# Hi and lo parts of the stationary weights interleaved, and activation blocks at a pitch of 2112 bytes

## The chip, the cores and the metric

The kernel runs on one core of one Trainium2 chip. The metric is the time of the kernel on the device in microseconds. Before the change it is 1505.89 us, the median of three runs (1504.97 to 1506.43).

## The reference

A decoder trunk of two layers over 512 positions and 1024 features, all in float32. Layer 0 mixes the tokens by dilated sliding-window attention in three groups of heads, layer 1 by a gated linear recurrence (RG-LRU). A gated ConvFFN follows each mixer, and every part stands between two RMS norms.

```python
def conv_ffn(x, w_up, conv_w, conv_b, w_down):
    u = causal_dwconv(x @ w_up, conv_w, conv_b)
    g, v = u[..., :D_FF], u[..., D_FF:]
    return (jax.nn.gelu(g, approximate=True) * v) @ w_down

for layer in range(DEPTH):
    h = rms_norm(x, norm_mix_pre[layer])
    h = attention(h) if layer % 2 == 0 else rglru_mixer(h)
    x = x + rms_norm(h, norm_mix_post[layer])
    h = conv_ffn(rms_norm(x, norm_ffn_pre[layer]), ...)
    x = x + rms_norm(h, norm_ffn_post[layer])
```

Nearly all of the arithmetic is in the products with the large weight matrices: `attn_w_qkv` (1024 x 9216), `attn_w_o`, `lru_w_in` (1024 x 2048), `lru_w_out`, and for each layer `ffn_w_up` (1024 x 6144) and `ffn_w_down` (3072 x 1024).

## The kernel before

**Split products.** To keep float32 accuracy at the pace of the type float32r, each operand is split into a part `hi`, which is the value rounded to float32r, and a part `lo`, the rest. `split` (line 145) does it for 512 columns at a time: ScalarE writes hi (line 146), and VectorE subtracts hi from the raw value and writes lo (line 147). A product is then three matmuls into the same bank of PSUM (`mm3`, line 245): hi with hi (line 246), hi with lo (line 247) and lo with hi (line 248). Each matmul loads its stationary operand, 128 x 128, anew; the profile lists these loads as LDWEIGHTS of the engine PEld. Small products, such as the scores of the attention, are plain float32 matmuls.

**Weights.** `plan` lists the chunks of the weights in the order of their use. `load` (line 187) fetches a chunk by DMA on SyncE's queue into one of three `raw` buffers, and `pump` (line 164) splits it into units of 128 x 1024, of which eight are alive at a time (`W_UNITS`). Until the change a unit is two tiles of the pool `wp`, tagged `hi` and `lo`, each of 4096 bytes in a partition. `pump` is called from `tick`, after every group of matmuls, and so the splits run ahead of the matmuls that use them. There are four kinds of unit:

- `feat`: 8 blocks of 128 input rows by 128 output columns. It is the stationary operand, and hT streams past it (`feat`, line 356): the result has features on the partitions and the 512 positions along the bank. It serves the queries and keys, `lru_w_in` and `ffn_w_up`: 80 chunks of two units, with 24 matmuls a unit (48 of 256 columns where the first tiles of a stage are done in halves).
- `gate`: the weights of the two gates of the recurrence, also stationary (`gates`, line 846); four units.
- `value`: two blocks of 512 columns. It streams, and hT is the stationary operand (`values`): the result v has positions on the partitions.
- `rows`: one block of 1024 columns. It streams, and the activation, split into `ahi` and `alo`, is stationary (`rows_run`, line 408): the result `acc` goes to the norms.

**Activations.** `new_hT` (line 277) makes the two tensors hT0 (hi) and hT1 (lo) in the pool `htp`: 8 blocks of 512 positions, 2048 bytes a block and 16384 bytes a tensor in each partition. `transposed` (line 293) fills them with the normed activation: TensorE transposes, ScalarE writes hi, VectorE writes lo.

**Other things on the path.** The attention's biases are laid out by GpSimd's queue: a row of biases goes to DRAM, is written 128 times over into `skew` there, and the `toe` tiles are read from it with a shifted pitch. In the recurrent layer `decay` is a chain of ScalarE, GpSimd and VectorE that ends in a scan; the projection that follows needs its result. The pools follow each other in the memory: `cp` (constants, the residual stream `x_sb`), then `htp`, `wp`, `gp` (28 general tiles of 2048 bytes) and `sp`.

Of the kernel before, what the change touches and what calls it, by code (L numbers as in the profile page):

```python
# [12 lines left out]
F32R = mybir.dt.float32r  # L13
# [5 lines left out]
P = 128  # L19
S = 512  # L20
D = 1024
KD = D // P
# [12 lines left out]
GEN_BUFS = 28  # L35
TOE_BUFS = 2
CP_PAD = 8

SHORT_ORDER = [
    ([0, 1], [0, 1, 2]), ([0], [3]), ([2, 3], [0]), ([1], [3]), ([2, 3], [1]), ([2], [2, 3]), ([3], [2, 3]),  # L40
# [36 lines left out]
def kernel(  # L77
# [29 lines left out]
    nc = tc.nc  # L107
    ctx.enter_context(tc.manual_schedule())
    cp = ctx.enter_context(tc.tile_pool(name="cp", bufs=1))
    cp.tile([P, CP_PAD], F32, tag="pad", name="pad")  # L110
    htp = ctx.enter_context(tc.tile_pool(name="htp", bufs=1))
    wp = ctx.enter_context(tc.tile_pool(name="wp", bufs=W_UNITS))
# [7 lines left out]
    def nm(s):  # L120
        uid[0] += 1
        return f"{s}{uid[0]}"
# [22 lines left out]
    def split(hi, lo, raw):  # L145
        nc.scalar.activation(hi, raw, AF.Copy)  # L146
        nc.vector.tensor_tensor(lo, raw, hi.bitcast(F32), op=ALU.subtract)  # L147

    plan = []
# [4 lines left out]
    def parts_of(kind, raw):  # L154

        if kind == "feat":
            return [raw[:, :, m * P : (m + 1) * P] for m in range(2)]
        if kind == "value":
            return [raw[:, 2 * i : 2 * i + 2, :] for i in range(2)]
        if kind == "rows":  # L160
            return [raw[:, i : i + 1, :] for i in range(2)]
        return [raw]

    def pump(limit=2):

        for _ in range(limit):
            i = state["cv"]
            if not pieces and i < state["dma"]:
                pieces.extend((i, j, u) for j, u in enumerate(parts_of(plan[i][0], raws.pop(i))))
                state["cv"] += 1  # L170
            if pieces and state["live"] < W_UNITS:
                i, j, raw = pieces.pop(0)
                hi, lo = (
                    wp.tile([P] + list(raw.shape[1:]), F32R, tag=t, name=nm("w" + t)) for t in ("hi", "lo")
                )
                h = raw.shape[1] // 2
                cuts = [(slice(None), slice(0, h)), (slice(None), slice(h, 2 * h))]
                if raw.shape[1] == 1:
                    cuts = [(slice(None), slice(0, 1), slice(n, n + 512)) for n in (0, 512)]
                for c in cuts:  # L180
                    split(hi[c], lo[c], raw[c])
                units[i, j] = (hi, lo)
                state["live"] += 1
            while not pieces and state["dma"] < len(plan) and state["dma"] - state["cv"] < RAW_BUFS:
                load()

    def load():
        i = state["dma"]
        kind, kd, cols, srcs = plan[i]
        raw = wp.tile([P, kd, cols], F32, tag="raw", name=nm("raw"), bufs=RAW_BUFS)  # L190
        at = 0
        for src, n in srcs:
            nc.sync.dma_start(raw[:, :, at : at + n] if kind == "value" else raw[:, at : at + n, :], src)
            at += n
        raws[i] = raw
        state["dma"] += 1
# [6 lines left out]
    def take(i, j):  # L203
        while (i, j) not in units:
            before = state["live"]
            pump(1)
            assert before != state["live"]
        return units[i, j]
# [7 lines left out]
    def tick():  # L216
        for s in list(sides):
            s[0] -= 1
            if s[0] <= 0:
                try:  # L220
                    s[0] = next(s[1])
                except StopIteration:
                    sides.remove(s)
        if not state["hold"]:
            pump(1 if state["live"] >= W_UNITS - 2 else 2)
# [49 lines left out]
        return [ap[:, 0:512], ap[:, 512:1024]]  # L275

    def new_hT():
        return tuple(htp.tile([P, KD, S], F32R, tag=f"hT{i}", name=nm(f"hT{i}")) for i in range(2))

    def prenorm(t, hT, g, wait):  # L280
        xh, gh = halves(x_sb[:, t, :]), halves(g)
# [126 lines left out]
    def rows_run(nchunks, A, prep, seq, order, post, pre):  # L408
        post_g = gain(*post)
        pre_g, hT = (gain(*pre), new_hT()) if pre is not None else (None, None)  # L410
        W, banks = {}, {}
        left = {}
# [93 lines left out]
    def ffn(layer, hT, post, pre):  # L506
        ca, cc = ffn_cols[layer]

        def conv(ps, j):
            u = gen(s="u")  # L510
            nc.scalar.activation(  # L511
                u, ps, AF.Identity, scale=cc[:, j : j + 1], bias=cc[:, 48 + j : 49 + j]
            )
            for d, wc in ((1, ca[:, 48 + j : 49 + j]), (2, ca[:, j : j + 1])):
                nc.vector.scalar_tensor_tensor(  # L515
                    u[:, d:], ps[:, : S - d], wc, u[:, d:], op0=ALU.mult, op1=ALU.add
                )
            return u

        gv = []  # L520

        def sink(b, ps, j):
            m = b % 2
            if b < 2:
                u = conv(ps, 2 * j + m)
                nc.scalar.activation(u, u, AF.Gelu_apprx_tanh)  # L526
                gv.append(u)
            else:
                u = conv(ps, 24 + 2 * j + m)
                nc.vector.tensor_tensor(gv[2 * j + m], gv[2 * j + m], u, op=ALU.mult)  # L530

        order = [([0, 1, 2, 3], range(9)), ([0], range(9, 12)), ([1], range(9, 12))]
        order += [([2, 3], [9]), ([2], [10, 11]), ([3], [10, 11])]
        prep, run = rows_proj(12, act_split(gv), order, post, pre)
        for j in range(12):
            if j == 11:
                prep(3)
            feat_tiles(2, hT, lambda b, ps: sink(b, ps, j), j == 0)
        return run()
# [286 lines left out]
    def lru(hT, post, pre):  # L826
# [40 lines left out]
        def decay(ns):  # L867

            js = [2 * n + m for n in ns for m in range(2)]
            at = {}  # L870
            for j in js:
                r = rs[j // 2][j % 2]
                a, th = gen(s="a"), gen(s="th")
                nc.scalar.activation(a, r, AF.Exp, scale=c8[:, j : j + 1])
                nc.scalar.activation(th, r, AF.Tanh, scale=c8[:, j : j + 1])
                nc.gpsimd.tensor_tensor(r, a, a, op=ALU.mult)
                at[j] = (a, th, r)
            for j in js:
                a, th, sq = at[j]
                nc.vector.scalar_tensor_tensor(th, sq, 1.0, th, op0=ALU.add, op1=ALU.mult)  # L880
                nc.vector.tensor_scalar(th, th, -1.0, 0.0, op0=ALU.mult, op1=ALU.max)
            pump(1)
            for j in js:
                nc.scalar.activation(at[j][1], at[j][1], AF.Sqrt)
            for j in js:
                a, th, _ = at[j]
                nc.vector.tensor_tensor(th, th, xb[j], op=ALU.mult)
                nc.vector.tensor_tensor_scan(th, a, th, 0.0, op0=ALU.mult, op1=ALU.add)
                hs.append(th)
                gate(j)  # L890
# [58 lines left out]

    root_table()  # L950
    hT = new_hT()
    nc.sync.dma_start(x_sb[:, 0, :], x[0, 0:P, :])
    g = gain(norm_mix_pre, 0, nc.sync)
# [27 lines left out]
    hT = attention(hT, (norm_mix_post, 0), (norm_ffn_pre, 0))  # L981
    hT = ffn(0, hT, (norm_ffn_post, 0), (norm_mix_pre, 1))
    hT = lru(hT, (norm_mix_post, 1), (norm_ffn_pre, 1))
# [30 lines left out]
```

## Time and profile before

| | |
|---|---|
| runs | 1504.97, 1506.43, 1505.89 us |
| profiled execution | 1504.94 us, of which the span of its instructions is 1503.2 us |
| granted clock of TensorE, mean | 0.995 |
| busy: TensorE, its weight loads | 1475.1 us, 1238.4 us |
| busy: VectorE, ScalarE, GpSimd | 799.3 us, 631.9 us, 53.8 us |
| moved by DMA | 157.65 MB, mean 105 GB/s |

The profile is one execution on the chip. A line of its groups gives the source line, the engine, the operation, what it writes and reads by the program's names without buffer numbers, the shape and the count; then the busy time in us and the mean of one in ns, and the idle time of the engine before them with what ended it. In the names, `ps<-hT,whi` is a matmul that writes the tile `ps` from hT and the hi part of a weight unit; `v<-whi,hT` and `acc<-whi,ahi` are the products of the `value` and `rows` kinds. Matmuls are pipelined: the duration of one reaches into the next, so the pace is read from the distance of their starts. In the timeline the first two columns are the start and the duration in us, and equal neighbours are merged with a count.

### The profile page before, as it was taken

The numbers are of one execution on the slowest core, as the hardware profiler recorded it, in microseconds if no ns is written. First come the engines' busy times: TensorE is split into PE (matmuls) and PEld (weight loads), VectorE is DVE, ScalarE is ACT, GpSimd is POOL, SyncE is SP. The second block draws the span as 40 slices with busy tenths as digits, with TensorE's granted clock in tenths as the row PEclk, the third lists the DMA queues.
The fourth block names the chain that finished last, engine by engine and source line by source line (L and its number), as shares of the span: only waits on it lengthen the run. The fifth ranks groups of instructions, "written<-read, shape, count | busy, mean of one in ns | idle before, by whom it ended". The sixth has DMA issues, their size and how long they took to land.

```text
span 1503.2 us, 18136 instructions
## 1 busy us (share of the span) xinstructions
PE 1475.1 (98%) x7083; PEld 1238.4 (82%) x7083; DVE 799.3 (53%) x1610; ACT 631.9 (42%) x1281; POOL 53.8 (4%) x81
## 2 busy tenths in 40 slices
PE   6999999999999999999999999999899999999998
PEld 4788888888888898888888888988698888888886
DVE  5434334343434686555565337868776555565333
ACT  5334333333333554344344234578554334444321
POOL 3021000000000000000000000003000000000000
PEclk9999999999999999999999999999999999999999
DMA  6543222424233324232233321252223232323301
GB/s 214 183 164 97 92 88 84 140 92 134 98 126 130 111 95 138 85 110 86 92 105 112 109 88 43 71 168 83 86 96 115 85 112 84 112 85 114 110 1 56
DMA packets 116102, 157.65 MB, mean 105 GB/s; under 512 B 5087, under 2 KB 97463, under 8 KB 116016
## 3 DMA queue, kind: packets, MB, share of 16 engines
q1 hardware_dynamic: 111120, 145.24, 29.1%
q0 software_dynamic: 4896, 11.26, 2.2%
q8 instruction: 55, 0.90, 0.3%
q14 instruction: 31, 0.25, 0.0%
HBM read 150.14 MB, written 11.05 MB: 107 GB/s over the span
## 4 chain that ended last, share of the span: by engine, by line
PE 95%; DVE 2%; issue 1%; DMA 1%; POOL 0%; ACT 0%; DVEq 0%; SPq 0%; POOLq 0%; ACTq 0%
PE ps L246 19%; PE ps L247 19%; PE ps L248 19%; PE acc L248 8%; PE acc L246 8%; PE acc L247 7%; PE v L246 3%; PE v L248 3%; PE v L247 3%; PE tr L297 1%; PE O L770 1%; PE S L712 1%; DVE wlo L147 1%; PE O L697 1%; PE S L662 1%
## 5 line engine op out<-in xcount | busy, mean ns | idle before, releaser
L246 PE MATMUL ps<-hT,whi 128*128 128x512 f32 (+1 forms) x1376 | 518.5, 377 | 0.0
L248 PE MATMUL ps<-hT,wlo 128*128 128x512 f32 (+1 forms) x1376 | 515.2, 374 | 0.0
L247 PE MATMUL ps<-hT,whi 128*128 128x512 f32 (+1 forms) x1376 | 515.1, 374 | 0.0
L147 DVE TENSOR_TENSOR wlo<-raw,whi 128x512 fp32r<-128x512 f32 x504 | 327.9, 697 | 276.5 <-ACT whi L146 276.3
L146 ACT ACTIVATE whi<-raw 128x512 fp32r<-128x512 f32 x504 | 285.0, 622 | 135.3 <-PE acc L248 120.9
L246 PEld LDWEIGHTS ps<-hT,whi 128*128 128x128 f32 x1376 | 259.1, 188 | 47.2 <-ACT qk L588 0.6
L248 PEld LDWEIGHTS ps<-hT,wlo 128*128 128x128 f32 x1376 | 259.0, 188 | 46.4
L247 PEld LDWEIGHTS ps<-hT,whi 128*128 128x128 f32 x1376 | 259.1, 188 | 45.6
L515 DVE SCALAR_TENSOR_TENSOR u<-ps,cols,u 128x511 f32<-128x511 f32 x192 | 143.8, 749 | 140.4 <-ACT u L511 137.0
L248 PE MATMUL acc<-whi,alo 128*128 128x512 f32 x512 | 200.0, 391 | 4.2 <-DVE alo L147 4.2
L246 PE MATMUL acc<-whi,ahi 128*128 128x512 f32 x512 | 200.6, 392 | 1.4 <-ACT ahi L146 1.4
L247 PE MATMUL acc<-wlo,ahi 128*128 128x512 f32 x512 | 199.7, 390 | 0.0
L511 ACT ACTIVATE u<-ps,cols 128x512 f32<-128x512 f32 x96 | 74.8, 780 | 209.8 <-PE ps L248 209.8
L248 PEld LDWEIGHTS acc<-whi,alo 128*128 128x128 f32 x512 | 96.5, 188 | 24.9 <-DVE alo L147 4.7
L246 PEld LDWEIGHTS acc<-whi,ahi 128*128 128x128 f32 x512 | 96.5, 188 | 21.5 <-ACT ahi L146 1.8
L247 PEld LDWEIGHTS acc<-wlo,ahi 128*128 128x128 f32 x512 | 96.4, 188 | 19.7
L247 PE MATMUL v<-wlo,hT 128*128 128x512 f32 x192 | 76.3, 398 | 3.3 <-DVE wlo L147 3.3
L246 PE MATMUL v<-whi,hT 128*128 128x512 f32 x192 | 78.0, 406 | 0.0
L248 PE MATMUL v<-whi,hT 128*128 128x512 f32 x192 | 75.9, 395 | 0.0
L526 ACT ACTIVATE u<-u 128x512 f32<-128x512 f32 x48 | 30.3, 632 | 80.7 <-DVE u L515 80.7
L649 DVE CUSTOM_DVE_ANT_0 L<-S,toe 128x128 f32<-128x128 f32 (+1 forms) x96 | 25.2, 321 | 52.7 <-DMA toe<-skew 21.9
L588 ACT ACTIVATE qk<-ps 128x512 f32<-128x512 f32 x24 | 14.3, 597 | 88.7 <-PE ps L248 76.9
(167 smaller groups left out, 1040.6 us busy)
## 6 DMA issues: line engine op xcount, KB each, us to landing
raw<-in_ffn_w_up_dram SPq DMA_DIRECT2D x48, 1024.0 KB, 5.2
raw<-in_attn_w_qkv_dram SPq DMA_DIRECT2D x28, 1024.0 KB, 5.0
raw<-in_ffn_w_down_dram SPq DMA_DIRECT2D x24, 1024.0 KB, 4.9
raw<-in_attn_w_qkv_dram SPq DMA_DIRECT2D x16, 512.0 KB, 4.9
raw<-in_lru_w_in_dram SPq DMA_DIRECT2D x8, 1024.0 KB, 5.5
skew<-rowv POOLq DMA_DIRECT2D x3, 1536.0 KB, 12.2
vrows<-v SPq DMA_DIRECT2D x16, 256.0 KB, 2.9
vp<-vrows SPq DMA_DIRECT2D x16, 256.0 KB, 4.2
```

The costliest lines, as they stand in the source:

```text
L146: nc.scalar.activation(hi, raw, AF.Copy)
L147: nc.vector.tensor_tensor(lo, raw, hi.bitcast(F32), op=ALU.subtract)
L246: mm(dst, l[0], r[0], start=start, stop=False)
L247: mm(dst, l[0], r[1], start=False, stop=False)
L248: mm(dst, l[1], r[0], start=False, stop=stop)
L297: nc.tensor.transpose(ps[:, k * P : (k + 1) * P], xs[i][:, k * P : (k + 1) * P], ident)
L511: nc.scalar.activation(u, ps, AF.Identity, scale=cc[:, j : j + 1], bias=cc[:, 48 + j : 49 + j])
L515: nc.vector.scalar_tensor_tensor(u[:, d:], ps[:, : S - d], wc, u[:, d:], op0=ALU.mult, op1=ALU.add)
L526: nc.scalar.activation(u, u, AF.Gelu_apprx_tanh)
L649: nc.vector.tensor_tensor_reduce(dst, ps, bias, scale=1.0, scalar=3 * NEG, op0=ALU.add, op1=ALU.max, accum_out=mx)
L662: mm(Sp[a // 2][:, o + lo : o + 256], q[hh][:, a * P : (a + 1) * P], k[hh][:, k0 : (a + 1) * P], start=True, stop=True)
L697: mm(po[:, a * P : (a + 1) * P], pts[a, j], vtile(v, a - 1 + j, h % 4), start=j == js[0], stop=j == 1)
```

## The change

Three edits. In `pump`, hi and lo of a unit become one tile of 8192 bytes. For the kinds `feat` and `gate` they alternate word by word: hi of column c lies at 8c bytes, lo at 8c + 4, and a block of 128 columns takes 1024 bytes. For `value` and `rows` hi fills the first half of the tile and lo the second, each in a row as before.

In `new_hT` the blocks of 512 positions stand 2112 bytes apart instead of 2048 (`HT_STEP`, 16 words). The second tensor gets another 1024 bytes at its end (`HT_GAP`, 256 words), so that both together take 34816 bytes, 17 times 2048, where they took 32768.

To make room, the memory that is set aside for the descriptors of GpSimd's DMAs is set to 8192 bytes.

```diff
+HT_STEP = 16
+HT_GAP = 256
...
             if pieces and state["live"] < W_UNITS:
                 i, j, raw = pieces.pop(0)
-                hi, lo = (
-                    wp.tile([P] + list(raw.shape[1:]), F32R, tag=t, name=nm("w" + t)) for t in ("hi", "lo")
-                )
+                n, m = raw.shape[1:]
+                both = wp.tile([P, 2 * n * m], F32R, tag="hl", name=nm("whl"))
+                if plan[i][0] in ("feat", "gate"):
+                    both = both.rearrange("p (k c t) -> p t k c", k=n, t=2)
+                else:
+                    both = both.rearrange("p (t k c) -> p t k c", k=n, t=2)
+                hi, lo = both[:, 0], both[:, 1]
...
     def new_hT():
-        return tuple(htp.tile([P, KD, S], F32R, tag=f"hT{i}", name=nm(f"hT{i}")) for i in range(2))
+        pitch = S + HT_STEP
+        both = []
+        for i in range(2):
+            t = htp.tile([P, KD * pitch + HT_GAP * i], F32R, tag=f"hT{i}", name=nm(f"hT{i}"))
+            both.append(t[:, : KD * pitch].rearrange("p (k s) -> p k s", k=KD)[:, :, :S])
+        return tuple(both)
...
-    nc = _bacc.Bacc("TRN2", target_bir_lowering=False, num_devices=1)
+    nc = _bacc.Bacc("TRN2", target_bir_lowering=False, num_devices=1, dynamic_dma_scratch_size=8192)
```

## The prediction, as it was put down before the result

> **What bounds the kernel now.** I read the page first: engines, chain, costliest groups. Then the groups by line with shapes kept apart, the timeline of one dense stretch, and the waits.
>
> ```profile
> span 1503.2 us, 18136 instructions
> PE 1475.1 (98%) x7083; PEld 1238.4 (82%) x7083; DVE 799.3 (53%) x1610; ACT 631.9 (42%) x1281; POOL 53.8 (4%) x81
> PE 95%; DVE 2%; issue 1%; DMA 1%; POOL 0%; ACT 0%; DVEq 0%; SPq 0%; POOLq 0%; ACTq 0%
> ...
> L147 DVE TENSOR_TENSOR wlo<-raw,whi 128x512 fp32r<-128x512 f32 x504 | 327.9, 697 | 276.5 <-ACT whi L146 276.3
> L146 ACT ACTIVATE whi<-raw 128x512 fp32r<-128x512 f32 x504 | 285.0, 622 | 135.3 <-PE acc L248 120.9
> ```
>
> TensorE carries 95% of the chain that ended last. VectorE and ScalarE have about half of the span free. So the change is worth what it does to the distance from one matmul's start to the next, and the durations don't give that, because matmuls overlap. The groups say which kinds there are, and the timeline gives the distance.
>
> ```profile
> L246 PE MATMUL ps<-hT,whi 128*128 128x512 f32 x1184 | 463.7, 392 | 0.0
> L248 PE MATMUL ps<-hT,wlo 128*128 128x512 f32 x1184 | 460.9, 389 | 0.0
> L247 PE MATMUL ps<-hT,whi 128*128 128x512 f32 x1184 | 460.8, 389 | 0.0
> ...
> L247 PE MATMUL v<-wlo,hT 128*128 128x512 f32 x192 | 76.3, 398 | 3.3 <-DVE wlo L147 3.3
> ...
> L246 PE MATMUL ps<-hT,whi 128*128 128x256 f32 x192 | 54.8, 285 | 0.0
> ...
> L246 PE MATMUL gate<-xhi,whi 128*128 128x512 f32 x32 | 12.4, 389 | 0.0
> ...
> L662 PE MATMUL S<-qk,qk 128*128 128x256 f32 x48 | 11.7, 380 | 0.0
> ```
>
> ```profile
> 203.68 1.14 ACT L146 ACTIVATE whi<-raw 128x512 fp32r<-128x512 f32 x2
> ...
> 203.96 0.39 PE L247 MATMUL ps<-hT,whi 128*128 128x512 f32 x1
> ...
> 204.19 0.39 PE L248 MATMUL ps<-hT,wlo 128*128 128x512 f32 x1
> 204.19 0.19 PEld L246 LDWEIGHTS ps<-hT,whi 128*128 128x128 f32 x1
> 204.34 1.29 DVE L147 TENSOR_TENSOR wlo<-raw,whi 128x512 fp32r<-128x512 f32 x2 [0.58 <-ACT whi L146]
> ...
> 206.23 0.39 PE L248 MATMUL ps<-hT,wlo 128*128 128x512 f32 x1
> ...
> 208.27 0.39 PE L248 MATMUL ps<-hT,wlo 128*128 128x512 f32 x1
> ...
> 208.50 1.72 PE L697 MATMUL O<-v,PT 128*128 128x128 f32 x14
> ```
>
> ```profile
> 940.02 0.28 PE L248 MATMUL ps<-hT,wlo 128*128 128x256 f32 x1
> ...
> 941.82 0.28 PE L248 MATMUL ps<-hT,wlo 128*128 128x256 f32 x1
> ```
>
> From 203.96 to 208.27 lie 19 distances: 0.2268 us each. From 940.02 to 941.82 lie 15: 0.120 us for 256 columns. The second 256 columns therefore cost 0.1068 us, 0.417 ns each, and what doesn't depend on columns is 226.8 - 213.6 = **13.2 ns in every matmul of a split pair**. The next weight load starts with the matmul (both 204.19) and lies inside it. This surplus is the only thing in the dense stretches that the change could take away.
>
> Is it fixed? Three places say no.
>
> ```profile
> 158.64 1.68 PE L662 MATMUL S<-qk,qk 128*128 128x128 f32 x8
> ```
>
> ```profile
> 27.74 0.63 PE L246 MATMUL v<-whi,hT 128*128 128x512 f32 x1
> ...
> 29.87 0.63 PE L248 MATMUL v<-whi,hT 128*128 128x512 f32 x1
> ```
>
> ```profile
> 27.10:30.50 3.40, 3.40 (x9) 2.72 (x9) 2.63 (x10) 1.29 (x3) 0.00 (x0) 0.50 0.00 0
> ```
>
> ```profile
> 281.51 0.40 PE L247 MATMUL ps<-hT,whi 128*128 128x512 f32 x1
> ...
> 283.59 0.39 PE L247 MATMUL ps<-hT,whi 128*128 128x512 f32 x1
> ```
>
> First, plain float32 matmuls. The 14 of 128 columns at 208.50 take (1.72 - 0.28) / 13 = 0.111 us each. The eight at 158.64 are two of 128 and six of 256; less the last one's 0.38 and two at 0.111, five remain: 0.216 us for 256 columns, which is 512 column times (213.6) and 2 ns. They stream at half the pace and pay 2, not 13. Second, at granted clock 0.50 (third figure from the end of the window's row) the split kind goes five distances in 2.13 us: 0.426 us, 512 columns at 0.833 ns with nothing left over; a fixed count of array cycles would have doubled instead. Third, after short matmuls the same instruction needs (283.59 - 281.51) / 9 = 0.231 us until it settles at 0.227. So the surplus appears only where 512 columns stream at full pace beside a weight load, and depends on how the two lie to each other: I read it as the load and the stream getting in each other's way. Against a general shortage of memory speaks that 203.96 to 206.23 (ACT and DVE at work) and 206.23 to 208.27 (neither) give the same distance.
>
> **The change part by part.**
>
> *Weights 8 bytes from column to column.* It touches the matmuls whose weights are whi or wlo: 3 x 1184 of 512 columns, 3 x 192 of 256, 3 x 32 gates; 3648 long and 576 short. The 128 weights now span 1024 bytes where they spanned 512, so a load walks through memory as many bytes per matmul column as the stream does, which is how the float32 matmuls lie (one weight column per moving column time). No row shows a weight load at this pitch. Upper bound of the gain: the surplus falls to the 2 ns of the float32 row, 226.8 to 215.6, so 3648 x 11.2 = 40.9 us; the short ones fall from 120 to the 111 ns at which loads follow each other in the L697 row, 576 x 9 = 5.2 us. Other end: the load now covers twice the bytes, and the surplus doubles, 4224 x 13.2 = 55.8 us lost. I take the first, being nearest to a row in which both walk at one pace; it stays the largest uncertainty.
>
> *Blocks at 2112 bytes, and a gap of 1024 behind the second tensor.* Every block of hT starts 64 bytes later against the weights than the one before. Stream and load of all kinds (ps, v, gate) now start at distances that are multiples of 512 bytes, and all settle at the same 0.227, so the trace can't tell what a shift does. The v matmuls, 576, use hT as weights at the old 4 bytes: between 0.231 (the unsettled row; +2.4 us) and 0.2156 (-6.5 us); I take nothing.
>
> *Strided writes and reads of the split.* Of the 504 weight splits 328 (80 column chunks x 4 and 4 gates x 2) now write, and on VectorE also read, every second word. The nearest rows:
>
> ```profile
> L776 ACT ACTIVATE oT<-O 128x512 f32<-128x512 f32 x8 | 8.8, 1100 | 39.7 <-PE O L770 34.0 <-issue 5.8
> ...
> L753 ACT ACTIVATE PT<-PT 128x512 f32<-128x512 f32 x16 | 8.6, 590 | 0.0
> ```
>
> Line 776 writes words 16 bytes apart and takes 1100 ns; line 753 writes them in a row, 590. So the price is between 0 and 510 ns a split, at most 328 x 0.51 = 167 us on ScalarE (then 799 of 1503) and as much on VectorE (then 966). The Trainium skill, "SBUF — State Buffer", section "Specifications (TRN2)", states 16-byte lines that need two hits each for full rate: by it the row at 16 bytes pays and a pitch of 8 does not, so 0. Either way it lies beside matmuls (columns: stretch, its length, then busy time and count of PE, PEld, DVE, ACT, POOL, then granted clock, DMA share, GB/s):
>
> ```profile
> 556.00:780.00 224.00, 224.00 (x1023) 186.94 (x1023) 131.16 (x192) 93.05 (x152) 0.00 (x0) 1.00 0.31 103
> ...
> 960.00:1070.00 110.00, 104.36 (x458) 85.83 (x457) 85.13 (x122) 76.13 (x120) 11.42 (x10) 0.98 0.35 115
> ```
>
> In the first ConvFFN (556 to 780) VectorE has 93 us free and DMA is at 0.31; matmuls faster by 5% need no more than that. In the recurrent layer (960 to 1070) TensorE idles 5.6 us because the chain of decay ends late there. Between the last gates and the projection stand three chunks, 144 matmuls: what they gain the wait takes back, 144 x 11.2 = 1.6 us. If that cover is gone, the eight to sixteen splits there cost up to 0.51 us each on VectorE, 4 to 8 us.
>
> *One tile for hi and lo.* A matmul that reads hi might now wait for lo's write too, one L147 (0.7 us) later. All of TensorE's later work would queue behind it; but units are prepared ahead, and TensorE's list of waits has none for the ps matmuls:
>
> ```profile
> PE tr L297 <- ACT xs L330: 10.3, 1, 10.3
> PE acc L248 <- DVE alo L147: 4.2, 1, 4.2
> PE v L247 <- DVE wlo L147: 3.3, 5, 0.7
> ```
>
> So 0. *The smaller scratch for DMA descriptors* touches POOL's queue. The three skew writes (1536 KB, 12.2 us to landing) are followed by the toe loads, for which VectorE waits 21.9 us and TensorE never. Queued behind them are the loads of the constants; I take 0.
>
> ```profile
> skew<-rowv POOLq DMA_DIRECT2D x3, 1536.0 KB, 12.2
> ...
> DVE L L649 <- DMA toe<-skew: 21.9, 2, 12.6
> ```
>
> **Sum**, against the profiled execution's 1504.94 (span 1503.2 and 1.7 around it): -40.9 - 5.2 + 1.6 = -44.5, so 1460.4. The median of the runs lies 0.95 above that execution: 1461.4, given as **1462**.
>
> **The rivals.**
>
> *The surplus doesn't depend on addresses.* What the load takes would be counted in columns, 128 whatever their pitch. For: it is equal in ps, v, gate. Against: all of these had like distances. Nothing moves: **1505**. The Trainium skill, "TensorE: Matmul & The Clock Gate", section "Step-by-step: what each phase is for", speaks for this and against the change: TensorE has two independent read ports, and loading the next weights takes no read bandwidth from the running matmul. The trace agrees that a load lies wholly inside a matmul, not that it is free: 13.2 ns remain at full pace.
>
> *Bytes touched are what counts* (the slower side). The surplus would be one piece per stretch of memory that the load opens; 1024 bytes instead of 512 double it from 13.2 to 26.4 in 4224 matmuls: 1504.9 + 55.8 + 1.0, **1561**. For: at clock 0.50 the surplus vanishes although load and stream slow down together, so their ratio of bytes is unchanged; a shortage of reading does that, a mismatch of paces alone does not. And strided access costs double in line 776. Against: ACT's and DVE's reading changes nothing. It decides as soon as the distance of ps matmuls lies above 0.2268.
>
> *Only the strided splits are felt*, TensorE's pace unchanged: the recurrent layer's 4 to 8 us, **1509 to 1514**.
>
> **How the numbers follow.** Surplus gone or mostly gone (half would be 1483): 0.45. No dependence: 0.27. Bytes touched: 0.16. Strided splits, or a shift that unsettles v (+2.4): 0.12. About 0.2% (3 us) can be told from no change. Faster is the first case and 0.03 of the second, 0.48; same 0.24; slower the last two, 0.28. The range takes in the first, second and fourth, 0.84, from 1457 (the upper bound with v's gain in part) to 1514. The likeliest case alone: 1457 to 1484.
>
> **What would show it.** Right: ps matmuls 0.216 apart in dense stretches, 0.111 to 0.112 for 256 columns, acc unchanged at 0.227, weight loads no longer than 0.19; L146 and L147 near 622 and 697. Wrong: 0.227 (no dependence), 0.240 (bytes touched), or L146 towards 1100 with TensorE waiting for whi. Also wrong, if v moves as much as ps: then the pitch of hT counted, not that of the weights.

## The result, and the profile after

The changed kernel takes **1525.45 us** (1524.93 to 1526.18, four runs) against 1505.83 us for the kernel before: a ratio of **1.0131**, 95% interval 1.0116 to 1.0146. It is slower by 19.6 us. The forecast was 1462 us, faster, with a range of 1457 to 1514.

The page of the changed kernel: engines, the chain that ended last, the weight splits.

```profile
span 1523.1 us, 18135 instructions
PE 1496.4 (98%) x7083; PEld 1264.5 (83%) x7083; DVE 799.4 (52%) x1610; ACT 642.1 (42%) x1281; POOL 54.0 (4%) x81
PE 95%; DVE 2%; issue 1%; DMA 1%; POOL 0%; ACT 0%; DVEq 0%; SPq 0%; POOLq 0%; ACTq 0%
...
L149 DVE TENSOR_TENSOR whl<-raw,whl 128x512 fp32r<-128x512 f32 x504 | 327.9, 697 | 281.9 <-ACT whl L148 281.5
L148 ACT ACTIVATE whl<-raw 128x512 fp32r<-128x512 f32 x504 | 296.2, 649 | 136.7 <-PE acc L254 120.9
L252 PEld LDWEIGHTS ps<-hT,whl 128*128 128x128 f32 x1376 | 267.5, 194 | 46.7 <-ACT qk L599 0.6
```

The span grew by 19.9 us and TensorE's busy time by 21.3, with the same count of matmuls, so TensorE idles no more than before. VectorE's time is the same, and ScalarE's 10 us more lie beside TensorE. So the matmuls themselves stand further apart. To see by how much, take 180 us of the first ConvFFN in which TensorE runs without a gap and only ps matmuls of 512 columns are issued. The window's row gives the stretch, its length, then busy time and count of TensorE; the first is of the kernel before, asked for TensorE alone, the second of the changed one, with PEld, DVE, ACT and POOL behind. At the end stand granted clock, DMA share and GB/s.

```profile
580.00:760.00 180.00, 180.00 (x796) 1.00 0.30 97
```

```profile
580.00:760.00 180.00, 180.00 (x777) 151.07 (x776) 101.13 (x148) 72.09 (x115) 0.00 (x0) 1.00 0.29 95
```

A matmul counts when its 0.39 us touch the window, so the distance is 180.39 / 796 = **226.6 ns** before and 180.39 / 777 = **232.2 ns** after. Over all starts of a kind in the trace, pauses (distances over 1.25 times the usual one) left out, the means are:

| distance in ns | count | before | after |
|---|---|---|---|
| ps, 512 columns | 3552 | 226.9 | 232.2 |
| ps, 256 columns | 576 | 119.8 | 119.8 |
| gate | 96 | 226.7 | 233.2 |
| v (hT is the weight) | 576 | 227.7 | 231.9 |
| acc (neither changed) | 1535 | 226.9 | 226.9 |

3552 x 5.3 + 576 x 4.2 + 96 x 6.5 = 21.9 us, close to the 21.3 us by which the busy time grew. The row of v matters: its weights are at 4 bytes as before, only the pitch of hT is new. The gates are the opposite: their stream is no part of hT, only their weights are new. Both got slower, so both halves of the change seemed to cost. How the distances follow each other inside a unit says more (medians by place in the unit, 24 places, worked out from the starts):

```
before  227 at every place
after   230 233 233 229 235 232 230 236 229 237 233 229 | 230 233 233 229 235 232 230 236 229 237 233 229
```

Before, a unit settles at one value. After, it runs through a pattern that comes back every 12 matmuls, which are four blocks; and over four blocks the stream moves by 4 x 64 = 256 bytes against the weights, if multiples of 1024 are left out.

### The profile page after: what moved, and what is told of

Its sections match the earlier page's. It is cut to its first block, busy times and chain, and to the rows that moved or that the text cites. A ratio compares the mean times of both kernels' runs of the same rounds, so it can differ in the third digit from the quotient of the medians.

```text
span 1523.1 us, 18135 instructions
## 1 busy us (share of the span) xinstructions
PE 1496.4 (98%) x7083; PEld 1264.5 (83%) x7083; DVE 799.4 (52%) x1610; ACT 642.1 (42%) x1281; POOL 54.0 (4%) x81
## 4 chain that ended last, share of the span: by engine, by line
PE 95%; DVE 2%; issue 1%; DMA 1%; POOL 0%; ACT 0%; DVEq 0%; SPq 0%; POOLq 0%; ACTq 0%
PE ps L253 19%; PE ps L252 19%; PE ps L254 19%; PE acc L254 7%; PE acc L252 7%; PE acc L253 7%; PE v L252 3%; PE v L253 3%; PE v L254 3%; PE tr L308 1%; PE S L723 1%; PE O L781 1%; DVE whl L149 1%; PE O L708 1%; PE S L673 1%
## 5 line engine op out<-in xcount | busy, mean ns | idle before, releaser
L252 PE MATMUL ps<-hT,whl 128*128 128x512 f32 (+1 forms) x1376 | 524.1, 381 | 0.0
L253 PE MATMUL ps<-hT,whl 128*128 128x512 f32 (+1 forms) x1376 | 522.1, 379 | 0.0
L254 PE MATMUL ps<-hT,whl 128*128 128x512 f32 (+1 forms) x1376 | 519.9, 378 | 0.0
L149 DVE TENSOR_TENSOR whl<-raw,whl 128x512 fp32r<-128x512 f32 x504 | 327.9, 697 | 281.9 <-ACT whl L148 281.5
L148 ACT ACTIVATE whl<-raw 128x512 fp32r<-128x512 f32 x504 | 296.2, 649 | 136.7 <-PE acc L254 120.9
L252 PEld LDWEIGHTS ps<-hT,whl 128*128 128x128 f32 x1376 | 267.5, 194 | 46.7 <-ACT qk L599 0.6
L253 PEld LDWEIGHTS ps<-hT,whl 128*128 128x128 f32 x1376 | 269.5, 196 | 43.5
L254 PEld LDWEIGHTS ps<-hT,whl 128*128 128x128 f32 x1376 | 268.8, 195 | 42.1
L254 PE MATMUL acc<-whl,alo 128*128 128x512 f32 x512 | 200.2, 391 | 4.2 <-DVE alo L149 4.2
L252 PE MATMUL acc<-whl,ahi 128*128 128x512 f32 x512 | 200.8, 392 | 0.5 <-ACT ahi L148 0.5
L253 PE MATMUL acc<-whl,ahi 128*128 128x512 f32 x512 | 199.8, 390 | 0.0
L254 PEld LDWEIGHTS acc<-whl,alo 128*128 128x128 f32 x512 | 96.6, 189 | 24.8 <-DVE alo L149 4.7
L252 PEld LDWEIGHTS acc<-whl,ahi 128*128 128x128 f32 x512 | 96.6, 189 | 20.8 <-ACT ahi L148 1.0
L253 PEld LDWEIGHTS acc<-whl,ahi 128*128 128x128 f32 x512 | 96.6, 189 | 19.8
L253 PE MATMUL v<-whl,hT 128*128 128x512 f32 x192 | 76.9, 401 | 2.8 <-DVE whl L149 2.8
L252 PE MATMUL v<-whl,hT 128*128 128x512 f32 x192 | 78.5, 409 | 0.0
L254 PE MATMUL v<-whl,hT 128*128 128x512 f32 x192 | 76.0, 396 | 0.0
```

Source lines behind the costliest of these rows:

```text
L252: mm(dst, l[0], r[0], start=start, stop=False)
L253: mm(dst, l[0], r[1], start=False, stop=False)
L254: mm(dst, l[1], r[0], start=False, stop=stop)
```

## The experiments

Two theories stood at first. **A**: weights at 8 bytes cost by themselves, because the load opens 1024 bytes instead of 512. **B**: the 64-byte steps of hT cost, because load and stream never settle.

**The halves of the change, each alone, and a control.** `interleave_only` keeps hT and the descriptor memory as before. `pitch_only` keeps hi and lo in a row, and `one_tile` does so with hT as before.

```diff
 # interleave_only
-HT_STEP = 16
-HT_GAP = 256
+HT_STEP = 0
+HT_GAP = 0
...
-... num_devices=1, dynamic_dma_scratch_size=8192)
+... num_devices=1)
 # pitch_only
-                if plan[i][0] in ("feat", "gate"):
+                if plan[i][0] in ():
 # one_tile: as pitch_only, and HT_STEP = 0, HT_GAP = 0
```

> Weights interleaved as in the changed kernel; hT at 2048 bytes and the descriptor memory as before. Theory A (the 8-byte weights themselves cost, because the load opens 1024 bytes instead of 512): ps matmuls 231 to 234 ns apart, v back at 227.7, the time 17 to 19 us above before, about 1523. Theory B (what costs is that the blocks of hT stand 64 bytes further against the weights at each step, so that load and stream never settle): ps at 227, only the 96 gate matmuls at 233, about 1506.

> hT at 2112 bytes with the gap and the smaller descriptor memory; hi and lo one after the other in one tile for all kinds of unit. Theory A: ps at 227, v at 232, so 2 to 3 us above before, about 1508. Theory B: ps and v at 231 to 233, about 1523, gates at 227.

> Control: only the one tile for hi and lo (one after the other) and the smaller descriptor memory, hT at 2048 bytes. Both theories: all split matmuls at 227, within 2 us of before, 1504 to 1508.

| kernel | us | ratio to before (95%) | ps | gate | v |
|---|---|---|---|---|---|
| interleave_only | 1533.34 | 1.0183 (1.0166 to 1.0200) | 234.9 | 235.6 | 227.9 |
| pitch_only | 1522.89 | 1.0115 (1.0100 to 1.0130) | 231.8 | 227.3 | 231.7 |
| one_tile | 1506.39 | 1.0003 (0.9994 to 1.0013) | 226.9 | 226.7 | 227.7 |

The same window, first of interleave_only, then of pitch_only:

```profile
580.00:760.00 180.00, 180.00 (x766) 150.21 (x765) 99.84 (x146) 70.34 (x112) 0.00 (x0) 1.00 0.30 96
```

```profile
580.00:760.00 180.00, 180.00 (x779) 145.93 (x778) 100.97 (x148) 69.92 (x116) 0.00 (x0) 1.00 0.29 95
```

766 and 779 matmuls where before had 796. Both theories are half right, and neither expected the whole: each half alone slows the kernel, by 27.9 and 17.5 us (A had expected 17 to 19 for the first, B 17 for the second), and both together cost 19.6, less than the interleaving alone. They don't add up. The short matmuls lose next to nothing: 120.0 ns with the interleaving alone, and 118.4 with the pitch alone. The one tile and the smaller descriptor memory cost nothing.

**A table of paces.** To see what the distance depends on, a small kernel leaves the trunk out and issues series of 24 split-type matmuls with the same two operands, from one tile.

```diff
+STEPS = (1, 2)
+OFFS = (0, 4, 8, 16, 24, 32, 48, 64, 80, 96, 112, 128, 160, 192, 224, 256, 384, 512)
...
+    def series(count, w_at, step, m_at):
...
+        for n in range(count):
+            w, m = w_at(n), m_at(n)
+            mm(ps, fill[:, w : w + 127 * step + 1 : step], fill[:, m : m + 512], start=n == 0, stop=n == count - 1)
...
+    M0 = 4096
+    same = lambda v: lambda n: v
...
+    for step in STEPS:
+        for off in OFFS:
+            series(24, same(0), step, same(M0 + off))
```

All of these count in words of 4 bytes: `w` and `m` are the starts of weights and stream, `step` the pitch of the weights.

> A kernel that leaves the whole trunk out: series of split-type matmuls of 512 columns from one tile, weights always at its start, 4 or 8 bytes from column to column, the stream at 18 starts of 16384 + 0 to 2048 bytes; then four series in the order of a ps unit (both weight pitches, blocks at 2048 and 2112). Theory A: every series at 4 bytes about 227 ns apart, every series at 8 bytes 230 to 240, whatever the start. Theory B: both pitches spread by more than 4 ns over the starts, and of the four unit series those with 2112 are slow. If neither start nor pitch matters in the table (all 227), the cost comes from changing addresses between one matmul and the next.

The timeline merges a series into one row: start, duration, count. The name of the target is the series; the granted clock is 1.00.

```profile
24.87 5.60 PE L129 MATMUL rab<-fill 128*128 128x512 f32 x24
30.31 5.72 PE L129 MATMUL rac<-fill 128*128 128x512 f32 x24
35.87 5.77 PE L129 MATMUL rad<-fill 128*128 128x512 f32 x24
...
52.58 5.76 PE L129 MATMUL rag<-fill 128*128 128x512 f32 x24
...
63.77 5.62 PE L129 MATMUL rai<-fill 128*128 128x512 f32 x24
...
85.93 5.62 PE L129 MATMUL ram<-fill 128*128 128x512 f32 x24
...
124.37 5.76 PE L129 MATMUL rat<-fill 128*128 128x512 f32 x24
...
224.79 16.49 PE L129 MATMUL rbl<-fill 128*128 128x512 f32 x72
241.11 16.86 PE L129 MATMUL rbm<-fill 128*128 128x512 f32 x72
257.81 16.95 PE L129 MATMUL rbn<-fill 128*128 128x512 f32 x72
274.60 16.89 PE L129 MATMUL rbo<-fill 128*128 128x512 f32 x72
```

A row's duration less the last matmul's 0.39, over 23 distances: with weights at 4 bytes and the stream 16384 + 0, 16, 32, 128, 256 and 512 bytes behind them (rab, rac, rad, rag, rai, ram) 226.5, 231.7, 233.9, 233.5, 227.4 and 227.4 ns. The two at 256 and 512 begin a little slower and settle at 226.7. So do those at 768, 1024, 1536 and 2048; every other start of the table, from 16 to 896 bytes, ends between 228.9 and 233.3. This is the new theory, **C: with weights at 4 bytes the pace depends on the distance of stream and weights modulo 256 bytes, and a multiple of 256 is the good case.** The kernel before has nothing but multiples of 512. At 8 bytes none of the 18 starts settled under 230.0, and most are at 233.3 (rat): A had this half of the table right, and the 4-byte half wrong. The last four rows are series of 72 in the order of a ps unit: 4 bytes with blocks at 2048 226.8 ns and at 2112 232.0; 8 bytes with 2048 233.2 and with 2112 232.4. These are the four kernels in small, in the same order, with nothing but TensorE at work. Only the interleaving alone is dearer in the kernel, 234.9 ns.

**C in the kernel itself.** If the 64 bytes hurt only because they are no multiple of 256, a larger step that is one should cost nothing.

```diff
 # pitch_2304: as pitch_only
-HT_STEP = 16
-HT_GAP = 256
+HT_STEP = 64
+HT_GAP = 0
```

> As the run with the pitch of hT alone, but the blocks 2304 bytes apart (256 more than 2048 instead of 64), weights at 4 bytes. Theory C (in the table the 4-byte series settle at 226.7 wherever the stream starts a multiple of 256 bytes from the weights, and at 229 to 233 in between: a pattern of 256 bytes): all distances stay multiples of 256, so ps and v at 227 and the time within 2 us of before, 1504 to 1508. Theory B (any shift of the blocks from one to the next unsettles them): about 1522, as with 2112.

1506.28 us, ratio 0.9999 (0.9989 to 1.0009). The window holds 796 matmuls again:

```profile
580.00:760.00 180.00, 180.00 (x796) 149.10 (x795) 102.39 (x149) 70.68 (x116) 0.00 (x0) 1.00 0.30 95
```

B falls: blocks 2304 bytes apart step against the weights from block to block too, and cost nothing. Two more kernels put C to the test: one with the interleaving, one without the gap.

```diff
 # both_2304: the changed kernel with HT_STEP = 64, HT_GAP = 0
 # pitch_no_gap: pitch_only with HT_GAP = 0
```

> The changed kernel with hT at 2304 bytes instead of 2112 and no gap: weights at 8 bytes, every distance of block and weights a multiple of 256 bytes as in the run with the interleaving alone. Theory C (distance modulo 256 and pitch of the weights decide): the same as the interleaving alone, ps at 235, 1531 to 1535, and so slower than the changed kernel, whose 64-byte steps vary the distance. If the larger pitch as such helped the changed kernel (1525): 1522 to 1527.

> hT at 2112 bytes without the 1024 bytes behind the second tensor, weights at 4 bytes one after the other. Theory C: 1024 is a multiple of 256, so the gap does nothing: the same as with it, ps at 231 to 232, 1521 to 1525. If the gap sets the distance that hurts: 1506 to 1515.

1532.14 us (1.0179, 1.0164 to 1.0194), and 1522.30 us (1.0111, 1.0094 to 1.0128), both as C has it. With hT at 2304 the interleaved kernel repeats the pattern of interleave_only place by place, 238 233 235 and so on; the 1024 bytes of the gap change nothing. So it is the 64-byte steps, not a larger pitch or the gap, that make the changed kernel better than its interleaving alone. They carry it through four distances modulo 256, and not all are equally bad for 8-byte weights: in the first table those series end at 233.3, 233.3, 231.7 and 230.0 ns for 0, 64, 128 and 192 bytes, 232.1 in the mean, where the changed kernel has 232.2. That this mixture is the reason is argued from the table and not shown in the kernel, whose interleaving alone has 234.9 where the table has 233.3.

**Is it the neighbourhood of hi and lo?**

```diff
 # blocks: as one_tile, but for the kinds feat and gate
-                    both = both.rearrange("p (k c t) -> p t k c", k=n, t=2)
+                    both = both.rearrange("p (k t c) -> p t k c", k=n, t=2)
```

> Control for the interleaving: hi and lo of the stationary kinds alternate by blocks of 128 columns (512 bytes hi, 512 bytes lo) in one tile, 4 bytes from column to column; hT at 2048 bytes, smaller descriptor memory. If the distance from column to column is what costs: ps and gate at 227, 1504 to 1508. If it is that hi and lo share a stretch of memory, or that blocks of the weights lie 1024 bytes apart: ps at 233 to 235, about 1530.

1506.04 us, 1.0003 (0.9993 to 1.0012), ps at 226.9. Hi and lo may share a tile and lie 512 bytes apart; what costs in the interleaving is the 8 bytes from column to column.

**What the load does to the stream.** Two more tables vary the size and the pitch of the load, and move the weights instead of the stream.

> A kernel that leaves the whole trunk out: more series of 24 split-type matmuls of 512 columns. If the surplus over 213.3 ns is taken by the weight load while it lasts (theory C), loads of 96, 64, 32 and 16 columns instead of 128 leave 10, 6.7, 3.3 and 1.7 ns at a distance of a multiple of 256 bytes, and in proportion to 20 ns at 128 bytes more; if it is a fixed price of changing weights, 13.3 remain with every size. Finer starts: by C only distances near 0 and 256 bytes reach 226.7; a start with less than 226 would be new and would give a faster kernel. Weights at 12, 16, 32 and 64 bytes: by theory A (bytes opened) the surplus grows with the pitch, up to four times at 16 bytes and no more after that. Both operands moved together by 4 to 128 bytes: by C no change from 226.7. A stream 64 KB away: by C the same as one 16 KB away.

> A kernel that leaves the whole trunk out: series of 24 split-type matmuls. First the stream stays and the weights (4 bytes) move by -256 to +256 bytes: if the distance between the two counts, 226.7 at -256, 0 and +256 and 229 to 234 between, as when the stream moved; if the start of the stream alone counts, 226.7 throughout. Then weights at 8 bytes, starting at word 0 or 1, with ten starts of the stream from 0 to 48 bytes: if 8 bytes can reach the pace of 4 bytes at all, some start gives 227 or less; I expect none under 229. Last, streams of 256, 384 and 448 columns: if the surplus arises while the load runs, it is the same for every width (13 ns at 4 bytes and distance 0, 16 to 21 otherwise); if it grows along the stream, it falls with the width.

Rows of the first, by the columns that a load has and the distance of the stream beyond 16384 bytes: rab 128 columns at 0, raf 64 at 0, raj 16 at 0; then, at 128 columns, raq with the stream 20 bytes further, rbo with weights at 12 bytes, rbq at 16, rbs at 32, and rbw with both operands moved by 4 bytes.

```profile
24.14 5.60 PE L128 MATMUL rab<-fill 128*128 128x512 f32 x24
...
46.27 5.68 PE L128 MATMUL raf<-fill 128*64 128x512 f32 x24
...
68.42 5.67 PE L128 MATMUL raj<-fill 128*16 128x512 f32 x24
...
107.30 5.92 PE L128 MATMUL raq<-fill 128*128 128x512 f32 x24
...
241.01 5.81 PE L128 MATMUL rbo<-fill 128*128 128x512 f32 x24
...
252.26 5.80 PE L128 MATMUL rbq<-fill 128*128 128x512 f32 x24
...
263.63 6.04 PE L128 MATMUL rbs<-fill 128*128 128x512 f32 x24
...
286.73 5.86 PE L128 MATMUL rbw<-fill 128*128 128x512 f32 x24
```

The loads of the same run, by group (mean ns of one after the busy time):

```profile
L128 PEld LDWEIGHTS rbs<-fill 128*128 128x128 f32 x24 | 5.9, 329 | 0.0
...
L128 PEld LDWEIGHTS rbq<-fill 128*128 128x128 f32 x24 | 5.7, 310 | 0.0
...
L128 PEld LDWEIGHTS rbo<-fill 128*128 128x128 f32 x24 | 5.7, 253 | 0.0
L128 PEld LDWEIGHTS rab<-fill 128*128 128x128 f32 x24 | 4.5, 188 | 0.9
...
L128 PEld LDWEIGHTS raj<-fill 128*16 128x16 f32 x24 | 2.3, 94 | 3.2
```

The expectation in proportion to the load missed: a load of 16 columns lasts 94 ns instead of 188, and its matmuls are 229.6 ns apart instead of 226.5. Nor does a fixed 13.3 remain: the shorter loads settle 15.6 to 18.4 ns above 213.3. Whatever the surplus over 213.3 is, it isn't in proportion to the words that the load reads. Theory A's count of bytes misses too: weights at 16 bytes open four times the memory of the ones at 4, and the surplus goes from 13 to 22 ns (5.80 - 0.39 over 23 is 235.2), not to 53; at 32 bytes it is 31 (rbs, 244.5 once settled), at 64 bytes 22 again. "No change when both move" missed for small moves: 4 bytes give 237.8 (rbw), 8 and 16 bytes 231 and 230, and only 32, 64 and 128 return to 226.7. So at 4 bytes the good case has two conditions, as far as tried: both moved by multiples of 32 bytes, and a distance that is a multiple of 256. A stream 64 KB away behaved as the one 16 KB away, as expected. Of 29 starts between 0 and 256 bytes none settled under 226.5; 28, 60 and 240 bytes reached 226.7 as well, so multiples of 256 are not the only good places, and the worst, 20 bytes, gave 240.0 once settled.

In the second table the stream stays and the weights move. That is mostly the same as moving the stream: 226.7 at distances that are multiples of 256, 228.9 at 64 bytes more, 231.7 to 233.3 at most others. But the two conditions are not the whole rule. Rows with the weights at -240 (rac), -16 (rai), +16 (raj) and +240 bytes (rap):

```profile
30.93 5.61 PE L128 MATMUL rac<-fill 128*128 128x512 f32 x24
...
64.26 5.66 PE L128 MATMUL rai<-fill 128*128 128x512 f32 x24
69.75 5.76 PE L128 MATMUL raj<-fill 128*128 128x512 f32 x24
...
103.22 5.60 PE L128 MATMUL rap<-fill 128*128 128x512 f32 x24
```

-240 and +16 lie alike modulo 256 and modulo 32, and settled at 226.7 and 233.3; so do -16 and +240, with 228.3 and 226.7. A longer pattern or the state that a series starts from would do this. For the state speaks that one series, the stream 128 bytes further, settled in two different patterns within one run of the other table (233.2 and 232.5 ns in the mean, after different neighbours); the runs don't decide it. Weights at 8 bytes gave 232.2 to 235.0 at all 20 fine starts. The widths gave this (four starts each, last 12 of a series; in brackets, at start 0, the surplus over 0.4167 ns a column, which is (173.3 - 120.0) / 128 from the table itself):

| columns | 4 bytes, start 0 | 4 bytes, other starts | 8 bytes, start 0 | 8 bytes, other starts |
|---|---|---|---|---|
| 256 | 120.0 (13.3) | 117.8 to 118.8 | 120.0 (13.3) | 118.3 to 121.1 |
| 384 | 173.3 (13.3) | 173.3 to 175.6 | 173.3 (13.3) | 173.3 to 175.0 |
| 448 | 202.4 (15.7) | 200.0 to 204.1 | 203.3 (16.7) | 200.0 to 206.7 |
| 512, all tables | 226.7 (13.3) | 226.7 to 240.0 | 233.3 (20.0) | 230.0 to 235.0 |

At start 0, 8 bytes have the surplus of 4 bytes up to 384 columns and a larger one only beyond; neither of the two expectations, equal at every width or falling with it, had that. The row of 256 columns in the result, which didn't move, fits: at that width all starts and both pitches lie between 117.8 and 121.1.

No arrangement of matmuls of 512 columns beat 226.5 ns, the pace of the kernel before, so the runs point to no faster version; the 1 to 2 ns in the 576 short matmuls (pitch_only has 1.4) would be worth 1 us. **Left open:** why the patterns have 256 bytes, and what it is between load and stream that depends on them. The runs show when the price changes, not the circuit that takes it. Nor was it followed further why the gates take 233.2 in one kernel and 235.6 in another at like distances, and why the interleaved ps matmuls take 234.9 in the kernel and 233.2 in the small table.

## Why the prediction was wrong

**What bounds the kernel** held: TensorE's distances set the time, and the whole change of 19.6 us came through them.

**The surplus** of 13.2 ns was read rightly, also that it isn't fixed. The runs confirm its dependence on how load and stream lie: moving the stream or the weights alone changes it, moving both by 32, 64 or 128 bytes doesn't. The third observation, 231 ns after short matmuls, was the one to take seriously: it showed that the same instruction can run worse than 227, and no row that was shown had a split matmul of 512 columns at full clock doing better.

**The weights at 8 bytes** are the step that failed. The prediction named two ends, 40.9 + 5.2 us gained and 55.8 us lost, and took the first as "nearest to a row in which both walk at one pace". That row, the plain float32 matmul, streams at half the pace, and so does the stretch at clock 0.50 that the prediction held against itself: two paces equal, or merely slow, look alike there. No row separated the two, so the step from equal paces to a surplus of 2 ns at full pace had nothing under it. What stood in its place was a surplus of 234.9 - 213.3 = 21.6 ns with the interleaving alone, and 18.9 in the changed kernel; a term that was to give 46.1 us cost 27.9 by itself.

**The rival "bytes touched"** had the sign right and the reason wrong: it wanted 240 ns and twice the surplus at every width; measured were 232.2 here, an unchanged 119.8 at 256 columns, and no proportion to bytes at 16 or 64. So "it decides as soon as the distance of ps matmuls lies above 0.2268" was too quick: the distance lay above, with another cause. The other sign, v moving as much as ps, did point at the pitch of hT (4.2 and 5.3 ns).

**"No dependence"** fell with the table: moving only the stream by 128 bytes takes the pace from 226.5 to 233.5. The Trainium skill, "TensorE: Matmul & The Clock Gate", section "Step-by-step: what each phase is for", has two independent read ports and says that loading the next weights takes no read bandwidth from the running matmul. The measurement differs from the first: load and stream are not independent. On the second the runs say only that a smaller load doesn't help.

**The blocks at 2112 bytes** were set at nothing, because "the trace can't tell what a shift does". That was true, and the value was wrong: alone they cost 17.5 us, nearly all in the ps matmuls (3552 x 4.9 ns). The bound of 0.231 that the prediction put on v nearly held (231.7 to 231.9), but it wasn't applied to ps, which have six times as many matmuls. With it the range would have reached 1505 + 3552 x 0.0042 + 2.4 = 1522, which is what pitch_only has. This is the second step that failed: a term set at nothing without a row for it.

**The splits** were bounded rightly: ScalarE's went from 622 to 649 ns in the mean, which is 27 x 504 / 328 = 41 ns for one that writes at 8 bytes, near the lower end, and VectorE's stayed at 697. The Trainium skill's two hits to a line ("SBUF — State Buffer", section "Specifications (TRN2)") let expect no price at 8 bytes. VectorE agrees, ScalarE nearly, and so do the loads above, 188 ns at 4 bytes and 194 at 8, but 253 at 12 and 310 at 16. The load at 8 bytes is hardly slower. The matmul beside it is. **One tile** and **the descriptor memory** at 0 held (one_tile).

## What to carry to other kernels

A trace in which every operand lies at the same distance says nothing on what a shift would do, and "nothing" is then no estimate; look for an unsettled stretch, and apply its price to all matmuls that the shift reaches. Where a stream of float32r with 512 columns runs beside weight loads, keep the weights dense and all bases and pitches of both at multiples of 256 bytes: the surplus was 13.3 ns a matmul there, and mostly 15 to 27 elsewhere at 4 and 8 bytes. Before a layout is changed in a large kernel, a series of 24 matmuls for each candidate, one row of the timeline each, prices it, here to within 2 ns a matmul.

## What the runs showed of the hardware that was not expected

- The distance of two split matmuls of 512 columns depends on addresses: 226.7 ns where weights (4 bytes from column to column) and stream lie a multiple of 256 bytes apart, mostly 229 to 235 elsewhere, 240.0 at 20 bytes; and moving both by 4 bytes gave 237.8.
- With weights 8 bytes from column to column, no start that was tried settled under 230.0 ns, while the load itself took 193 to 196 instead of 188.
- Most series that settle to one distance have 226.7, 233.3 or 240.0 ns, which are 13.3, 20.0 and 26.7 over the time of 512 columns; one (44 bytes) has 230.0. The others run through patterns of two or more matmuls whose means mostly lie between.
- A load of 16 columns instead of 128 lasts half as long and doesn't shorten the distance.
- Two causes that each slow the kernel, by 27.9 and 17.5 us, cost 19.6 together.
